# Last 256 tokens of the closing FFN as rows, and a reordered first layer, in a two-layer streaming encoder step

## The chip, the cores and the metric

The kernel runs on one core of one Trainium2 chip. The metric is the device time of one execution in microseconds (us); the time before is the median of 3 runs, 1388.47 us (1387.64 to 1388.97). The profile shows one execution, of 1387.13 us, whose span from the first to the last instruction is 1385.4 us.

The core's engines have queues of their own and wait for each other by semaphores: PE (matrix products; its weight loads are shown as PEld), DVE (vector), ACT (scalar and table functions), POOL, and SP, which here only issues DMAs. Each works its instructions off in the order in which the program wrote them.

## What is computed

576 tokens of 1024 features (64 of a running stream, then 512 of a new one) go through two layers. Layer 0 is a mixer of two head groups, mLSTM and retention, behind one input projection; layer 1 is a latent attention. Each is followed by a SwiGLU FFN, and after every sub-layer stands a norm of the residual. Cut to what matters here:

```
def layer(x):
    x = layer_norm(ALPHA * x + mixer(x), g_mix, b_mix)
    return layer_norm(ALPHA * x + swiglu(x), g_ffn, b_ffn)

def mixer_ab(x):                      # layer 0
    mq, mk, mv, mo, mif, rq, rk, rv, rg = split(x @ w_in)
    h = mlstm(mq, mk, mv, gates(mif))     # per chunk of tokens, state carried on
    o = retention(rope(rq), rope(rk), rv) # the same
    return concat(head_norm(h) * sigmoid(mo), head_norm(o) * silu(rg)) @ w_out

def swiglu(x):
    g, u = split(x @ w_gu)
    return (silu(g) * u) @ w_down
```

All is float32. The norm subtracts the mean over the 1024 features, divides by the root of the variance, and applies gain and bias.

## The kernel before

**Products.** A product is split into three: with each operand as a high and a low part in the rounded 32-bit type, it is high x high, low x high and high x low. So each weight and each activation exists twice (`Xh`, `Xl` for the input of a stage, `H` with its high and low halves for the input of a down or output projection). ACT writes the high part by a cast (L364), DVE the low part by a subtraction (L362).

**Weights.** The class `Plan` lays all weight pieces one after the other into blocks of 128 x 1024 (512 KB). SP brings a block into one of three raw buffers (`dma_w`, L342; a fourth is there for the FFN's own blocks); a block is called in as soon as a raw buffer's old contents have been split. Half a block (512 columns) is a *fill*: it is split into a ring *slot* when its order comes. That order is made by `prefetch(i, lead)`: whenever the program is about to use fill i, it first writes the splits of the fills up to i + lead, as far as their blocks are called in and a slot is free. Some fills have a slot of their own (`pins`). Since each engine works in program order, a split that is ordered early also stands early in the queues of ACT and DVE, ahead of what is written later.

**Order of the work.** It is written out by the program itself: main units of products follow each other, and between them `tick()` lets background tasks (norms, recurrences) emit their next step when a modelled PE clock has reached their due time (`LAG`).

**Token halves and tiles.** Feature-major products (`fm`) hold 320 or 256 tokens as columns (`HN`): weights stand, activations stream, and the output has features as partitions. Token-major products (`tm`) take a tile of 128 tokens (64 for the first) as the standing operand and stream 512 weight columns. Results come into PSUM banks: 3 for main products (`mm`), 4 for side work (`x`), 1 more (`o`).

**The first layer up to the mLSTM.** `setup` orders x of the first 320 tokens into `Z` and the first weight blocks: tiles 0 and 1 of x singly, then pairs. `layer0` splits x (L600, L601) and runs tiles 1 and 2 of the projection rq,rk as x arrives. x of the other 256 tokens is ordered at k = 3 and 4, after the constants (L752 to L754: rope, identity, mask, and the gate weights). At k = 7 that second half is split, ahead of the evacuations with rope of tiles 1 and 2 (`ev_qk`, L697 to L704). Then come gate products of the first half, tile 0 and tile 3 of rq,rk, gate products of the second half, tile 4, and the token-major projections rv and mv. `gates` (L829 to L911) works out the mLSTM's stabilisers in steps, with transposes on PE in between, and ends with four small products that spread the decays. `retention` works tile by tile in three steps: scores times a decay mask (`s1`, L928), output and state update, then the norm over each head (`s2`, L950 to L970), and transposes of the result (`s3`). `s1` uses the one `o` bank and an `mm` bank. The feature-major projections from `mk` on begin when the last `s3` has been written. All ten slots of `L0_SLOTS` are shared by the projections' fills, and rq,rk's eight are held until its last tile.

**The end.** The closing FFN works its inner dimension in three parts (8, 7 and 7 tiles of 128); the last part's down projection runs as eight feature units per half (`down_units`), of 7 x 3 products each, five units of the first half ahead of the second's first (`chain`). Each unit's bank is added to `Z` (L1187). The norm works on features as partitions: an early mean estimate by a product with ones (`ln_c`), sums and squares per unit (L1209 to L1233), then statistics by products, a root by seven small DVE steps (L539 to L543), a diagonal matrix to spread it (L1261), and per feature tile a subtraction, a scaling and a bias (L1265, L1279, L1298, L1321). The tail of the second half shares this among DVE, ACT and POOL, and stores (L1283).

Of the kernel before, what the change touches and what calls it, by code (L numbers as in the profile page):

```python
# [42 lines left out]
FILL = 512  # L43
SKEW = 5
# [4 lines left out]
L0_SLOTS = (0, 1, 2, 3, 4, 5, 6, 7, 14, 15)  # L49
# [63 lines left out]
def weight_pieces():  # L113
# [58 lines left out]
class Plan:  # L172
# [4 lines left out]
    def __init__(self):  # L177
        self.blocks, self.fills, self.where, self.quads, self.quad_blocks = [], [], {}, {}, set()
        used, at, left = BLK, FILL, 0
        for p in weight_pieces():  # L180
# [23 lines left out]
            self.where[p[0]] = (len(self.fills) - 1, at, w)  # L204
            used += w
# [12 lines left out]
class Kern:  # L218
    def __init__(self, ctx, tc, t):
# [18 lines left out]
        self.done, self.late_lo = set(), None  # L238
        for li in range(2):
# [86 lines left out]
    def slot(self, s):  # L326
        b = self.buffer(s)
# [97 lines left out]
    def prefetch(self, i, lead, qlead=QLEAD):  # L425
        last = len(self.plan.fills) - 1
        self.load()
        while True:
# [3 lines left out]
            if j > min(i + (lead if j > last or len(self.plan.fills[j]) == 3 else qlead), last):  # L432
                return
# [120 lines left out]
    def setup(self):  # L554
# [42 lines left out]
    def split_x(self, half, ks):  # L597
        for k in ks:
            a, b = hcols(half, k)
            self.nc.scalar.copy(self.Xh[:, a:b], self.Z[:, a:b])  # L600
            self.nc.vector.tensor_tensor(self.Xl[:, a:b], self.Z[:, a:b], self.Xh[:, a:b].bitcast(F32), ALU.subtract)  # L601
# [20 lines left out]
    def layer0(self):  # L622
# [41 lines left out]
        def tm_units(name, evac, tiles=range(NT)):  # L664
# [72 lines left out]
        banks = [None, self.bank(), self.bank()]  # L737
        for k in range(KT):
# [16 lines left out]
            if k in (3, 4):  # L755
                j = k - 3
                nc.sync.dma_start(half_view(Z, 1, 4 * j, 4 * j + 4), half_dram(t["x"], 1, 4 * j, 4 * j + 4))
# [5 lines left out]
        tm_units("rqrk", ev_qk, (0,))  # L763
        tm_units("rqrk", ev_qk, (3,))
# [3 lines left out]
        tm_units("rqrk", ev_qk, (4,))  # L768
        tm_units("rv", ev_rv)
# [9 lines left out]
        tm_units("mv", ev_mv)  # L779
# [1484 lines left out]
```

## Time and profile before

| | |
|---|---|
| median of 3 runs | 1388.47 us (1387.64 to 1388.97) |
| profiled execution | 1387.13 us |
| its span | 1385.4 us |
| busy: PE, DVE, ACT, POOL | 97%, 71%, 44%, 11% of the span |
| PE waits for DVE T L1226 (late in the span) | 3.8 us in two waits |
| PE waits for ACT Z L1318 (norms between stages) | 3.6 us in two waits |
| DMA | 112.91 MB, mean 81 GB/s |

A row of the timeline gives the start in us, the duration, engine, line of the kernel, operation, the output and inputs by their names in the program, their shape, and how many instructions of one kind follow each other; in brackets stands the idle time of the engine before them and what ended it. A row of the waits gives who waited for whom, us in total, how often, and the longest. A row of the windows gives a stretch, its length, then busy time and instructions of PE, PEld, DVE, ACT and POOL, the clock that PE was granted, and share and rate of DMA. A row of the DMA table gives the count, the size, and the median us from issue to landing. The ends of matmuls are modelled.

### The profile page before, as it was taken

The numbers are of one execution on the slowest core, as the hardware profiler recorded it, in microseconds if no ns is written. First come the engines' busy times: TensorE is split into PE (matmuls) and PEld (weight loads), VectorE is DVE, ScalarE is ACT, GpSimd is POOL, SyncE is SP. The second block draws the span as 40 slices with busy tenths as digits, with TensorE's granted clock in tenths as the row PEclk, the third lists the DMA queues.
The fourth block names the chain that finished last, engine by engine and source line by source line (L and its number), as shares of the span: only waits on it lengthen the run. The fifth ranks groups of instructions, "written<-read, shape, count | busy, mean of one in ns | idle before, by whom it ended". The sixth has DMA issues, their size and how long they took to land.

```text
span 1385.4 us, 24616 instructions
## 1 busy us (share of the span) xinstructions
PE 1348.3 (97%) x9759; PEld 1302.8 (94%) x9759; DVE 978.6 (71%) x2277; ACT 612.1 (44%) x1295; POOL 154.8 (11%) x182
## 2 busy tenths in 40 slices
PE   8999999999999999999999999999999999999995
PEld 6778999999999999999988899999999999999995
DVE  6666777678873685588898666667787358647877
ACT  4422333445551453255355466644555135425533
POOL 1100001115000000000021533311310000000000
PEclk9999999999999999999999999999999999999997
DMA  6111122511232123222322011130313312222221
GB/s 219 61 62 60 53 65 64 191 60 62 91 107 78 62 99 113 78 92 91 123 85 60 31 31 32 31 107 31 92 62 115 100 62 92 92 92 77 94 75 69
DMA packets 38235, 112.91 MB, mean 81 GB/s; under 512 B 5025, under 2 KB 12513, under 8 KB 38121
## 3 DMA queue, kind: packets, MB, share of 16 engines
q1 hardware_dynamic: 38120, 111.35, 24.4%
q8 instruction: 76, 1.25, 0.4%
q14 instruction: 39, 0.31, 0.1%
HBM read 107.45 MB, written 3.89 MB: 80 GB/s over the span
## 4 chain that ended last, share of the span: by engine, by line
PE 81%; DVE 12%; ACT 3%; DMA 2%; issue 2%; POOL 0%; SPq 0%; POOLq 0%; ACTq 0%; DVEq 0%
PE mm L465 42%; PE x L465 36%; DVE r L362 2%; PE x L533 2%; DVE Z L1279 1%; DMA raw<-in_w 1%; DVE Z L1265 1%; PE o L465 1%; ACT r L364 1%; ACT Xh L1311 1%; ACT Z L1318 0%; DMA Z<-in_x 0%; DVE small L543 0%; DVE small L542 0%; DVE small L541 0%
## 5 line engine op out<-in xcount | busy, mean ns | idle before, releaser
L465 PE MATMUL mm<-H,r 128*128 128x320 f32 (+2 forms) x2832 | 386.5, 296 | 0.0
L465 PEld LDWEIGHTS mm<-H,r 128*128 128x128 f32 x2832 | 377.2, 188 | 0.5 <-issue 0.2
L465 PE MATMUL x<-Xh,r 128*128 128x288 f32 x1216 | 244.7, 295 | 0.0
L465 PE MATMUL mm<-Xh,r 128*128 128x288 f32 (+2 forms) x1152 | 230.3, 298 | 6.0 <-DVE Z L1185 2.9
L364 ACT CAST r<-raw 128x512 fp32r<-128x512 f32 (+2 forms) x292 | 178.6, 648 | 104.9 <-PE mm L465 75.9
L362 DVE TENSOR_TENSOR r<-raw,r 128x512 fp32r<-128x512 f32 (+2 forms) x276 | 194.4, 734 | 37.7 <-ACT r L364 37.5
L465 PE MATMUL x<-r,r 128*128 128x288 f32 (+2 forms) x1534 | 211.7, 293 | 0.2 <-DVE r L1055 0.2
L465 PEld LDWEIGHTS x<-r,r 128*128 128x128 f32 x1534 | 205.9, 188 | 0.7 <-DVE r L1055 0.5
L465 PEld LDWEIGHTS x<-Xh,r 128*128 128x128 f32 x1216 | 194.5, 188 | 0.5
L465 PEld LDWEIGHTS mm<-Xh,r 128*128 128x128 f32 x1152 | 184.5, 190 | 7.2 <-ACT Z L1318 3.8
L465 PE MATMUL x<-Xl,r 128*128 128x288 f32 x608 | 179.2, 295 | 0.0
L465 PE MATMUL mm<-Xl,r 128*128 128x288 f32 (+2 forms) x576 | 167.5, 299 | 0.0
L364 ACT CAST r<-T 128x512 fp32r<-128x512 f32 (+1 forms) x114 | 87.1, 764 | 127.8 <-DVE T L397 109.1
L465 PEld LDWEIGHTS x<-Xl,r 128*128 128x128 f32 x608 | 114.0, 188 | 0.0
L362 DVE TENSOR_TENSOR r<-T,r 128x512 fp32r<-128x512 f32 (+1 forms) x114 | 96.3, 866 | 19.0 <-ACT r L364 19.0
L465 PEld LDWEIGHTS mm<-Xl,r 128*128 128x128 f32 x576 | 107.8, 190 | 0.1
L465 PE MATMUL mm<-r,Xh 128*128 128x512 f32 (+1 forms) x320 | 97.1, 385 | 4.4 <-DVE r L699 1.8
L1319 POOL TENSOR_TENSOR Xl<-Z,Xh 128x288 fp32r<-128x288 f32 (+2 forms) x36 | 30.9, 861 | 466.9 <-ACT Z L1318 466.4
L465 PEld LDWEIGHTS mm<-r,Xh 128*128 128x128 f32 x320 | 57.6, 188 | 17.3 <-issue 2.2
L1223 ACT ACTIVATE T<-Z 128x288 f32<-128x288 f32 (+2 forms) x56 | 24.9, 445 | 91.5 <-DVE Z L1185 47.1
L465 PE MATMUL mm<-r,Xl 128*128 128x512 f32 (+1 forms) x160 | 60.5, 378 | 0.0
L1580 DVE TENSOR_TENSOR T<-T,x 128x288 f32<-128x288 f32 x38 | 17.3, 454 | 58.7 <-PE x L465 58.7
(316 smaller groups left out, 1723.3 us busy)
## 6 DMA issues: line engine op xcount, KB each, us to landing
raw<-in_w SPq DMA_DIRECT2D x169, 512.0 KB, 3.5
r<-in_w SPq DMA_DIRECT2D x20, 512.0 KB, 3.5
Z<-in_x SPq DMA_DIRECT2D x1, 1280.0 KB
o_y<-Z SPq DMA_DIRECT2D x2, 640.0 KB, 3.3
Z<-in_x SPq DMA_DIRECT2D x2, 512.0 KB, 6.2
Z<-in_x SPq DMA_DIRECT2D x1, 1024.0 KB, 8.8
o_y<-Z SPq DMA_DIRECT2D x4, 256.0 KB, 2.1
Z<-in_x SPq DMA_DIRECT2D x3, 320.0 KB, 4.7
```

What stands on the lines that cost most here:

```text
L362: self.lo_engine.tensor_tensor(t[:, 1], src, t[:, 0].bitcast(F32), ALU.subtract)
L364: self.nc.scalar.copy(t[:, 0], src)
L465: self.nc.tensor.matmul(out, lhsT, rhs, start=start, stop=stop, skip_group_check=more)
L533: self.nc.tensor.transpose(out, in_, self.ident[0:n, 0:n])
L1223: nc.scalar.activation(q, z, AF.Square)
L1265: V.tensor_tensor(z, z, xd[:, 0:n], ALU.subtract)
L1279: V.scalar_tensor_tensor(z, z, gain(m), R[:, 0:n], ALU.mult, ALU.mult)
L1311: A.activation(self.Xh[:, a:b], z, AF.Identity, bias=bias(m))
L1319: G.tensor_tensor(self.Xl[:, a:b], z, self.Xh[:, a:b].bitcast(F32), ALU.subtract)
L1580: V.tensor_tensor(s[:, 0:n], s[:, 0:n], ps, ALU.add)
```

## The change

Eight things are changed.

1. The last down projection's second half (256 tokens) is computed by rows. Its weights are laid out as 14 pieces of 512 columns (`dt`), which the first half's feature units read in parts of 128. All eight units of the first half run first. Then two tiles of 128 tokens follow, each in two groups of 512 features: four plain float32 products with the identity put the residual from `Z` into the bank, and 21 products add to it. The norm of the row tile is taken straight from the banks: statistics by BN_STATS, mean subtracted on ACT, scaling and bias by DVE (the first tile's bias by POOL). Gain and bias come by a DMA that repeats 8 KB on all partitions (1 MB). The output has an array of its own.
2. In this stage the fills are ordered eight ahead (`FILLS_T`).
3. x of the first half comes in single tiles up to tile 3, and the second weight block in two parts; x of the second half is ordered at k = 1, ahead of the constants, into a free tile.
4. Tiles 1 and 2 of rq,rk are evacuated before the second half of x is split.
5. The fills of rq,rk and mv get eight slots in `H`; a cap (`self.cap`) spreads how far ahead fills are ordered: rv's during rq,rk, mv's during rv, mk's during mv.
6. The gates' decay products come 4.5 later on the modelled clock.
7. In the retention the scores of tile i + 2 come between output and norm of tile i, and the second tile's scores use an `x` bank instead of `o`.
8. `mk` begins when the last `s2` has been written, not the last `s3`.

```diff
+FILLS_T = 8
-L0_SLOTS = (0, 1, 2, 3, 4, 5, 6, 7, 14, 15)
+L0_SLOTS = (6, 7, 14, 15, 0, 1, 2, 3, 4, 5)
...
+            if (li, f1) == (1, FT):
+
+                for g in range(2):
+                    for k in range(f0, f1):
+                        out.append(((("dt", g), k), "w_down", li, k * 128, [(512 * g, 512)]))
+                continue
...
+        for k in range(KT):
+            for nm in ("rqrk", "mv"):
+                self.pins[self.where[(nm, k)][0]] = (len(RING) + k,)
...
+        if s >= len(RING):
+            o = 2 * FILL * (s - len(RING))
+            return self.H[:, o:o + 2 * FILL].rearrange("p (e c) -> p e c", e=2)
...
-            if j > min(i + (lead if j > last or len(self.plan.fills[j]) == 3 else qlead), last):
+            if j > min(i + (lead if j > last or len(self.plan.fills[j]) == 3 else qlead), last, max(i, self.cap)):
...
-            for k in (2 * j, 2 * j + 1) if j == 0 else (2 * j,):
-                e = k + 1 if j == 0 else k + 2
+            for k in (2 * j, 2 * j + 1) if j < 2 else (2 * j,):
+                e = k + 1 if j < 2 else k + 2
                 nc.sync.dma_start(half_view(self.Z, 0, k, e), half_dram(t["x"], 0, k, e))
                 if j < RAW and k % 2 == 0:
-                    self.dma_w(j, 2 if j == 0 else 1)
+                    self.dma_w(j, 2 if j < 2 else 1)
...
+                    self.cap = self.where[(name, KT - 1)][0] + ahead * (1 if len(tiles) == 1 else i + 1)
...
         for k in range(KT):
-            self.lead = 1 - k % 2 if k < KT - 1 else LEAD
+            self.lead = 1 - k % 2
             self.split_x(0, [k])
             if k == KT - 1:
                 self.split_wg()
-                self.split_x(1, range(KT))
...
-                if k == KT - 1:
-                    ev_qk(i, banks[i])
-            if k == 3:
+            if k == 1:
+                for j in range(2):
+                    nc.sync.dma_start(x1[:, 4 * j:4 * j + 4, :], half_dram(t["x"], 1, 4 * j, 4 * j + 4))
                 for name in ("rope", "ident", "mask", "cst"):
...
+        for i in (1, 2):
+            ev_qk(i, banks[i])
+            self.split_x(1, range(4 * i - 4, 4 * i), x1)
...
         gate_mm(0)
-        tm_units("rqrk", ev_qk, (0,))
-        tm_units("rqrk", ev_qk, (3,))
+        self.lead = 2 * KT
+        tm_units("rqrk", ev_qk, (0,), 2)
+        tm_units("rqrk", ev_qk, (3,), 5)
         gate_mm(1)
...
-        tm_units("rqrk", ev_qk, (4,))
-        tm_units("rv", ev_rv)
+        tm_units("rqrk", ev_qk, (4,), 8)
+        tm_units("rv", ev_rv, ahead=2)
...
-        tm_units("mv", ev_mv)
+        tm_units("mv", ev_mv, ahead=2)
+        self.cap, self.lead = len(self.plan.fills), LEAD
...
-                self.wait(lambda: self.ret_at["s3"] == NT)
+                self.wait(lambda: self.ret_at["s2"] == NT)
...
+        yield 4.5
+        x3 = self.xbank()
+        for h in range(4):
+            self.mm(x3[:, h * 8:h * 8 + 5], self.sel[:, h * 128:(h + 1) * 128], dec, True, True)
...
-            for o, bank in enumerate((self.obank(), self.bank())):
+            for o, bank in enumerate((self.xbank() if i == 1 else self.obank(), self.bank())):
...
-            s2(i)
+            O = s2(i)
+            if i + 2 < NT:
+                s1(i + 2)
+            s2b(i, O)
...
-        self.chain(down_units(p, f0, f1), ahead)
+        if not last:
+            self.chain(down_units(p, f0, f1), ahead)
+            return
+
+        gb, rows = (self.st(x, [128, KT * NTOK]) for x in ("Xh", "Xl"))
+        nc.sync.dma_start(gb[:, 0:2048], self.t["lnt"].to_broadcast([128, 2048]))
+        gb = gb[:, 0:2048].rearrange("p (e f) -> p e f", e=2)
+        self.rel, self.lead = False, FILLS_T
+        for _, d in down_units(p, f0, f1):
+            d(0)
+            self.tick()
+        for i in range(2):
...
+            banks = [self.bank(), self.obank() if i else self.bank()]
+            for g, ps in enumerate(banks):
+                for j in range(4):
+                    z = (4 * g + j) * NTOK + c
+                    self.mm(ps[:, 128 * j:128 * j + 128], Z[:, z:z + 128], self.ident, j == 0, False, more=True)
+                for k in range(f0, f1):
+                    wh, wl = self.wget((("dt", g), k))
+                    o = (k - f0) * NTOK + c
+                    xh, xl = H[:, o:o + 128], H[:, LO + o:LO + o + 128]
+                    self.mm(ps, xh, wh, False, False, more=True)
+                    self.mm(ps, xh, wl, False, False, more=True)
+                    self.mm(ps, xl, wh, False, k == f1 - 1, more=True)
+                    if k % 2:
+                        self.tick()
+                V.bn_stats(bs[:, g, :], ps)
+            V.bn_aggr(mv, bs)
+            V.tensor_scalar(nm, mv[:, 0:1], -1.0, None, ALU.mult)
+            y = [rows[:, (2 * i + g) * 512:(2 * i + g + 1) * 512] for g in range(2)]
+            for g, ps in enumerate(banks):
+                A.activation(y[g], ps, AF.Identity, bias=nm)
+            V.tensor_scalar(ve, mv[:, 1:2], LN_EPS, None, ALU.add)
+            self.rsqrt(rs, ve, None, tt)
+            for g in range(2):
+                V.scalar_tensor_tensor(y[g], y[g], rs, gb[:, 0, 512 * g:512 * g + 512], ALU.mult, ALU.mult)
+                (V if i else G).tensor_tensor(y[g], y[g], gb[:, 1, 512 * g:512 * g + 512], ALU.add)
+                nc.sync.dma_start(self.t["o_yt"][i, :, 512 * g:512 * g + 512], y[g])
```

More of the change, by code (lines that the diff above doesn't have):

```diff
@@ L204, in __init__ @@
             self.where[p[0]] = (len(self.fills) - 1, at, w)
+            if p[0][0][0] == "dt":
+                for j in range(4):
+                    self.where[(("d", 1, 4 * p[0][0][1] + j), p[0][1])] = (len(self.fills) - 1, at + 128 * j, 128)
             used += w
@@ L238, in __init__ @@
         self.done, self.late_lo = set(), None
+        self.cap = len(self.plan.fills)
+        for k in range(KT):
+            for nm in ("rqrk", "mv"):
+                self.pins[self.where[(nm, k)][0]] = (len(RING) + k,)
         for li in range(2):
@@ L595, in split_wg, with split_x @@
         self.nc.vector.tensor_tensor(self.wgp[:, :, 8:16], wg, hi.bitcast(F32), ALU.subtract)
-    def split_x(self, half, ks):
+    def split_x(self, half, ks, src=None):
         for k in ks:
             a, b = hcols(half, k)
-            self.nc.scalar.copy(self.Xh[:, a:b], self.Z[:, a:b])
-            self.nc.vector.tensor_tensor(self.Xl[:, a:b], self.Z[:, a:b], self.Xh[:, a:b].bitcast(F32), ALU.subtract)
+            x = self.Z[:, a:b] if src is None else src[:, k, :]
+            self.nc.scalar.copy(self.Xh[:, a:b], x)
+            self.nc.vector.tensor_tensor(self.Xl[:, a:b], x, self.Xh[:, a:b].bitcast(F32), ALU.subtract)
     def xs(self, half, cut=HN[0]):
@@ L662, in layer0, with tm_units @@
         half_sum = Z[0:64, 3972:4484]
-        def tm_units(name, evac, tiles=range(NT)):
+        def tm_units(name, evac, tiles=range(NT), ahead=LEAD):
             for i in tiles:
@@ L737, in layer0 @@
         banks = [None, self.bank(), self.bank()]
+        x1 = T1[:, 0:KT * HN[1]].rearrange("p (k t) -> p k t", k=KT)
         for k in range(KT):
-            self.lead = 1 - k % 2 if k < KT - 1 else LEAD
+            self.lead = 1 - k % 2
             self.split_x(0, [k])
@@ L901, in gates @@
         V.tensor_copy(dec[:, 1:5], stk[32:36, 191::128])
-        x1, x2, x3 = self.xbank(), self.xbank(), self.xbank()
+        x1, x2 = self.xbank(), self.xbank()
         for i in range(1, NT):
@@ L905, in gates @@
         self.transpose(x2[0:64, 0:128], stk[:, 0:64])
-        for h in range(4):
-            self.mm(x3[:, h * 8:h * 8 + 5], self.sel[:, h * 128:(h + 1) * 128], dec, True, True)
         nc.gpsimd.memset(self.tc_[:, 0], 0.0)
@@ L959, in s2, with s2b @@
                         V.scalar_tensor_tensor(to, up, dec, to, ALU.mult, ALU.add)
+            return O
+        def s2b(i, O):
+            L = TLEN[i]
             bs = self.smalls(24).rearrange("p (h c) -> p h c", h=4)
@@ L987, in task @@
         def task(i):
-            while at["s1"] < i or at["s2"] < i - 1 or self.qk_done < NT:
-                yield
-            s1(i)
-            at["s1"] += 1
-            yield LAG["r1"]
+            if i < 2:
+                while at["s1"] < i or self.qk_done < NT:
+                    yield
+                s1(i)
+                at["s1"] += 1
+                yield LAG["r1"]
             while at["s2"] < i or at["s3"] < i - 1:
@@ L1668, in ffn @@
         self.use_slots(RING)
-        self.chain(down_units(p, f0, f1), ahead)
+        if not last:
[9 more added lines that the diff above has]
+        for i in range(2):
+            c = HN[0] + 128 * i
+            bs = self.smalls(12).rearrange("p (g c) -> p g c", g=2)
+            mv = self.smalls(2)
+            nm, ve, tt, rs = (self.smalls(1) for _ in range(4))
+            banks = [self.bank(), self.obank() if i else self.bank()]
+            for g, ps in enumerate(banks):
+                for j in range(4):
+                    z = (4 * g + j) * NTOK + c
[21 more added lines that the diff above has]
+                nc.sync.dma_start(self.t["o_yt"][i, :, 512 * g:512 * g + 512], y[g])
     def layer1(self):
@@ L2225, in host_inputs @@
     d["lnv"] = ln.transpose(3, 0, 1, 2)
+    d["lnt"] = np.concatenate([a["ln_ffn_g"][1], a["ln_ffn_b"][1]])[None, :]
     d["gq"] = np.concatenate([a["g_q"][0], a["g_kv"][0]])[None, :]
@@ L2234, in host_outputs @@
     import numpy as np
-    y = np.concatenate([r["o_y"][:, :8 * 320].reshape(128, 8, 320), r["o_y"][:, 8 * 320:].reshape(128, 8, 256)], 2)
-    y = y.transpose(2, 1, 0).reshape(NTOK, D_MODEL)
+    y = np.concatenate([r["o_y"].reshape(128, 8, 320).transpose(2, 1, 0).reshape(320, D_MODEL),
+                        r["o_yt"].reshape(256, D_MODEL)], 0)
     out = [y[64:], y[:64]]
```

5 lines of the change are left out of this document (1 added, 4 removed).

## The prediction

> **What bounds the kernel now.** I read the page first, then the waits of PE, then the timeline of PE at both ends of the program, since the change touches only the first 125 us and the last 65.
>
> ```profile
> span 1385.4 us, 24616 instructions
> PE 1348.3 (97%) x9759; PEld 1302.8 (94%) x9759; DVE 978.6 (71%) x2277; ACT 612.1 (44%) x1295; POOL 154.8 (11%) x182
> ```
>
> PE carries a record for 97% of the span, so there are only two ways to gain: less matmul work, or fewer of the 37 us in which PE has nothing. The waits of PE say where those are (us in total, times, longest):
>
> ```profile
> PE o L465 <- DVE r L928: 2.7, 2, 1.4
> PE mm L465 <- DVE r L699: 1.8, 1, 1.8
> PE mm L465 <- DVE r L362: 1.4, 2, 1.2
> PE mm L465 <- ACT r L364: 1.2, 1, 1.2
> PE x L533 <- DVE r L702: 0.4, 1, 0.4
> PE mm L533 <- DVE r L970: 0.3, 1, 0.3
> ```
>
> All six lie in the first layer. The rest is the tail, where the timeline of PE and of ACT (start, duration) shows:
>
> ```profile
> 1320.14 9.40 PE L465 MATMUL mm<-H,r 128*128 128x320 f32 x63
> 1329.38 0.32 PE L465 MATMUL x<-Z,ones 128*128 128x320 bf16 x1
> 1354.30 5.21 PE L465 MATMUL mm<-H,r 128*128 128x256 f32 x42
> 1359.35 0.78 PE L465 MATMUL x<-T,ones 128*128 128x128 f32 x6
> 1359.93 7.70 PE L465 MATMUL mm<-H,r 128*128 128x256 f32 x63
> 1379.99 1.80 ACT L1298 ACTIVATE Z<-Z,lnv 128x256 f32<-128x256 f32 x4 [0.88 <-POOL Z L1291]
> ```
>
> The last product ends at 1359.93+7.70 = 1367.6. The span ends at 1385.4, so 17.8 us follow in which the last half is normed on DVE, POOL and ACT and stored; of these 1385.4-1381.8 = 3.6 us come after the last ACT operation (the store).
>
> **The end: rows instead of columns.** The half of 256 tokens keeps its multiply work but turns it: 8 units x 21 products of 256 columns become 2 tiles x 2 groups x 21 products of 512. The 42 products from 1354.30 to 1359.35 take 0.120 us each, so 168 cost 20.2 us. A 512-wide product is seen in the first layer, and so are the plain f32 products that bring the residual into the bank by the identity (two records each):
>
> ```profile
> 67.46 0.63 PE L465 MATMUL mm<-r,Xh 128*128 128x512 f32 x2
> 67.93 0.39 PE L465 MATMUL mm<-r,Xl 128*128 128x512 f32 x1
> 68.16 0.63 PE L465 MATMUL mm<-r,Xh 128*128 128x512 f32 x2
> 84.83 1.05 PE L465 MATMUL x<-T,r 128*128 128x128 f32 x8
> 85.81 0.71 PE L465 MATMUL x<-T,Z 64*128 64x128 f32 x8
> ```
>
> Between 67.46 and 68.16 lie three products: 0.233 each, so 84 cost 19.6 us. Four plain products of 128 columns take 85.81-84.83 = 0.98, so 16 cost 3.9 us. (The six records at 1359.35, three products in 0.58, give 0.19 each and 3.1 us: the low bound.) PE's last product therefore moves by 19.6+3.9-20.2 = +3.3, to 1370.9. The statistics products of the other half's norm stay as they are.
>
> What follows the last product becomes short: one BN_STATS over 512, an aggregate, a negated mean, eps and the seven steps of the root, then four 512-wide operations and the store. ACT's two mean subtractions run beside the root.
>
> ```profile
> 88.49 0.88 DVE L964 BATCH_NORM_STATS2 small<-x 64x6 f32<-64x128 f32 x4
> 89.40 0.38 DVE L966 BATCH_NORM_AGGREGATE small<-small 64x2 f32<-64x6 f32 x4
> 90.01 0.16 DVE L539 TENSOR_SCALAR small<-small 64x4 int32<-64x4 int32 x1
> 91.16 0.16 DVE L543 SCALAR_TENSOR_TENSOR small<-small 64x4 f32<-64x4 f32 x1
> 25.25 0.69 DVE L697 TENSOR_TENSOR r<-mm,rope 128x512 f32<-128x512 f32 x1
> ```
>
> BN_STATS over 512 isn't in the trace: no less than one of 128 (0.22), no more than four (0.88); I take 0.65, near the 0.69 of the 512-wide row. Aggregate 0.1, negation 0.2, root and eps 0.2+(91.32-90.01) = 1.5, four operations at 0.69 less overlap 2.7, hand-over from PE 0.1 (an estimate): 5.3. With the store's 3.6 the tail is 8.9 instead of 17.8. Net: 8.9-3.3 = 5.6 us gained, 5.4 to 6.8 by these bounds. The other half's norm now hides under the row tiles, which last 19.6+3.9 = 23.5 us; the first row tile's norm and POOL's two bias adds hide under the second.
>
> Against it stands the order of the 14 splits. The lead of 8 puts all of them on ACT and DVE before the first product of the stage, so ahead of the first evacuation, and the 1 MB broadcast of gain and bias is put on the SP queue ahead of the last weight block.
>
> ```profile
> L342 SPq DMA_DIRECT2D raw<-in_w x1: 328/328/328, 1324.6 to 1324.6; - x1
> 1325.04 2.42 ACT L364 CAST r<-raw 128x512 fp32r<-128x512 f32 x4 [1.47 <-DMA raw<-in_w]
> 1326.31 0.88 DVE L1187 TENSOR_TENSOR Z<-Z,mm 128x320 f32<-128x320 f32 x2
> 1336.63 1.29 DVE L362 TENSOR_TENSOR r<-raw,r 128x512 fp32r<-128x512 f32 x2 [0.25 <-ACT r L364]
> 1294.00:1296.00 2.00, 2.00 (x17) 2.00 (x16) 2.00 (x4) 0.00 (x0) 0.00 (x0) 1.00 0.95 387
> raw<-in_w SPq DMA_DIRECT2D x169, 512.0 KB, 3.5
> ```
>
> Today the last block is issued at 1324.6 (it waits until splits 6 and 7 have read their buffer), its two splits run at 1336.6, and the first two evacuations go ahead of them at 1326.3. Afterwards they go behind. The block lands at 1324.6+3.5 = 1328.1 without the broadcast; blocks 4 and 5 land about 1325 to 1326 by the ACT row, the broadcast takes 1.05 MB at 387 GB/s = 2.7, the block 1.4 more: about 1330.2 with it. Two splits (0.6 of ACT until DVE can follow, a quarter of 2.42, then 1.3) and one evacuation (0.5) end at 1330.5 or 1332.6. PE wants that evacuation at 1329.38 (the mean product of the norm). It waits 1.1 to 3.2 us; I take 2.8, since the broadcast is issued first. [...] The end gives 5.6-2.8 = 2.8.
>
> **The first layer.** x by single tiles: today the third tile's products wait 1.2 for its weights. Smaller pieces bring tiles 2 and 3 earlier, but the gate products follow directly behind tile 7, and their weights now land later.
>
> ```profile
> 16.80 0.25 ACT L594 CAST wgp<-T 128x64 fp32r<-128x64 f32 x1 [2.02 <-DMA T<-in_wg]
> 17.08 0.23 DVE L595 TENSOR_TENSOR wgp<-T,wgp 128x64 fp32r<-128x64 f32 x1 [1.11 <-ACT wgp L594]
> 18.66 0.31 PE L465 MATMUL x<-Xh,wgp 128*16 128x320 f32 x1
> 15.00:20.00 5.00, 5.00 (x27) 3.72 (x26) 1.46 (x4) 0.95 (x4) 1.03 (x2) 1.00 0.88 265
> ```
>
> On the queue 1 MB of x (second half) now precedes the gate weights where a 0.5 MB block did: 0.52 MB at 387 to 265 GB/s is 1.4 to 2.0 us, so the gate weights are ready at 18.7 to 19.3 instead of 17.3. The gain at the start is swallowed: -0.1 (bounds -0.6 to 0).
>
> What goes: the two evacuations with rope no longer stand behind the split of the late second half of x (L699 1.8, L702 0.4). rqrk's weights get slots in H, so rv's eight splits are done before rv starts (the 1.2 of L362; its other 0.2 stays). The scores of tile i+2 precede the norm of tile i on DVE, so their bank is emptied before the norm, and the second tile gets its own bank (L928 2.7). mk starts without the last norm (L970 0.3). Sum 6.4. A wait counts from the modelled end of the last record. Two 512-wide records take 0.63 and the second starts 0.233 after the first, so one is 0.40 long, and the next could have started 0.16 before its end: 0.16 more for each of six, together 7.4.
>
> What comes: eight splits and the second half of x now stand in DVE's queue ahead of the gates' first stage, whose result ten transposes wait for.
>
> ```profile
> 19.73 1.43 DVE L601 TENSOR_TENSOR Xl<-Z,Xh 128x256 fp32r<-128x256 f32 x4 [2.43 <-ACT Xh L600]
> 37.48 0.42 DVE L704 TENSOR_TENSOR Z<-r,cst 128x256 f32<-128x256 f32 x1
> 39.85 0.16 DVE L829 TENSOR_TENSOR small<-x,bif 64x8 f32<-64x8 f32 x1 [1.96 <-issue]
> 42.96 0.18 DVE L849 TENSOR_TENSOR small<-small 128x20 f32<-128x20 f32 x1
> 45.27 1.24 PE L533 MATMUL x<-ident,small 64*4 64x64 f32 x10
> 85.00:120.00 35.00, 33.73 (x207) 27.86 (x207) 28.85 (x125) 4.72 (x9) 0.35 (x2) 1.00 0.00 1
> ```
>
> The four evacuations (first row at 25.25, above) take 25.25 to 37.90 = 12.65 without a gap. After the change DVE starts them at 18.7, and 2.9 of x and 8x0.65 = 5.2 of splits come between: 39.4, and with the gates' 3.3 (39.85 to 43.14) 42.7. PE arrives at the transposes at 45.27 less the waits gone by then (1.8+0.4 and 0.3 of uncounted) = 42.3 to 42.8 with the 0.1 above: a wait of 0.4 (0 to 2). The decay products, 4.5 later, are needed only by the mLSTM: nothing. First layer: 7.4-0.4-0.1 = 6.9.
>
> **Sum.** 6.9+2.8 = 9.7. The profiled execution took 1387.13 (span 1385.4 and 1.7 around it), so 1377.4; the median of the runs lies 1.34 above it: 1388.47-9.7 = **1378.8**.
>
> **The rivals.** *DVE becomes the bound of the first layer.* From 85 to 120 it is busy 28.85 of 35. The change takes one wait on L928 (1.4) out of that stretch and puts six to eight early splits (3.9 to 5.2) in: 32.8 to 34.0 in 33.6. Then the state update of the fourth tile comes too late for the fifth, and about 3 of the 7.4 come back as waits: 1381.8. For it speaks the fullness of DVE, against it that PE has a whole tile of mv (24x0.233 = 5.6) between two retention steps to run ahead.
>
> *The rows give nothing.* The wait for the last block is 5.6 rather than 2.8, if the broadcast runs at half the rate of weights: 1388.47-6.9 = 1381.6. No wide broadcast of this size is in the trace.
>
> *The early order doesn't happen.* A fill is skipped when its block has not been called in or its slot is held; then rv still waits 1.4 with its uncounted part: 1380.1. For it: there are still three raw buffers for blocks; against it, eight slots more.
>
> *Slower: the splits dam up the vector queue.* A split ordered ahead of its block's landing stops DVE, and the evacuation behind it. In the first layer 13 tiles order splits at their start, with three raw buffers. If each stop lasts d, 13d less the 6.1 of free DVE time above must exceed 9.7+2.8 before the kernel is slower by 0.2%: from d = 1.4 on. A landing takes 3.5. With d = 2, 26-6.1-9.7 = +10.2: 1398.7. Against it: mostly two splits, one block's worth, are ordered per tile, and the two other buffers can fill meanwhile.
>
> **How the numbers follow.** My forecast 0.50, DVE bound 0.23, rows give nothing 0.12, no early order 0.07, slower 0.06; 0.02 remains for better than forecast. The range reaches down to all waits gone and the upper bound of the end with no stop (1388.47-7.4-6.8 = 1374.3) and up to both middle rivals together, 1388.47-3.9 = 1384.6: 1374.5 to 1385.0. About 0.2% (2.8 us) is what a measurement tells from no change. Faster by more 0.87, within 0.07 (rivals adding up), slower 0.06.
>
> **What would show it.** Right: the waits on L699, L928 and L970 are gone, and the one on L362 is at most 0.2; the gate products start at 18.6 to 19.3; PE's last product ends about 1366.8 (1370.9+2.8-6.9) and 8.9 us follow it; one wait of 1 to 3 us on DVE Z early in the last stage. Wrong: a longer tail than 11 us, plain products dearer than 0.25, waits of the retention products on DVE updates, a wait over 4 on the last blocks, or PE idle at the row tiles.

## The result and the profile after

The changed kernel takes 1378.85 us (median of 4 runs, 1377.22 to 1379.03) against 1388.72 us (4 runs) for the kernel before on the same chip: ratio 0.9928, 95% interval 0.9916 to 0.9940, about 9.9 us less. The forecast was 1378.8. The sum came out; its two large terms did not.

First the page of the changed kernel, then its waits of PE (us in total, times, longest). Line numbers are now those of the changed kernel.

```profile
span 1377.0 us, 24436 instructions
PE 1348.6 (98%) x9692; PEld 1302.6 (95%) x9692; DVE 971.5 (71%) x2251; ACT 606.2 (44%) x1283; POOL 154.7 (11%) x180
```

```profile
PE x L482 <- DVE Z L1219: 3.7, 1, 3.7
...
PE x L550 <- DVE small L871: 0.5, 1, 0.5
PE x L482 <- DVE wgp L612: 0.3, 1, 0.3
```

All six waits that the prediction listed are gone from the first layer, but for twice 0.2 on splits of weights (L379, L381), of the kind that was expected to stay. Two small ones are new there (the gate transposes, the gate weights), and one large one in the last stage. The windows from the first product of the input projection to the first product of mk show the first layer, before and then after (start and end, length, then busy time of PE, PEld, DVE, ACT, POOL):

```profile
4.87:122.34 117.47, 109.64 (x568) 85.10 (x569) 83.56 (x254) 40.59 (x80) 9.39 (x24) 1.00 0.29 94
```

```profile
4.93:112.39 107.46, 106.31 (x564) 84.95 (x565) 84.42 (x244) 41.67 (x84) 9.19 (x24) 1.00 0.36 119
```

PE without a record fell from 117.47-109.64 = 7.8 to 1.15 us, and PE's recorded time by 3.3 more. Of the 10.0 some 0.5 is only moved (the last transposes of the retention now lie behind mk's start). The last stage begins at 1311.25 instead of 1320.14, so 8.9 us earlier. But from there to the end of the span it takes 1377.0-1311.25 = 65.75, where it took 65.26. **The rows gave nothing; the first layer gave all of it.** The timeline of PE in the last stage of the changed kernel shows where the rows' gain went:

```profile
1311.25 9.40 PE L482 MATMUL mm<-H,r 128*128 128x320 f32 x63
1324.31 0.42 PE L482 MATMUL x<-Z,ones 128*128 128x320 bf16 x1 [3.67 <-DVE Z L1219]
1324.34 18.26 PE L482 MATMUL mm<-H,r 128*128 128x320 f32 x105
1342.43 1.05 PE L482 MATMUL mm<-ident,Z 128*128 128x128 f32 x8
1343.24 2.34 PE L482 MATMUL mm<-r,H 128*128 128x512 f32 x9
...
1363.12 5.15 PE L482 MATMUL o<-r,H 128*128 128x512 f32 x21
```

PE stands for 3.67 us (3.84 with the uncounted part) at the first evacuation. The 63 products ahead of it start 0.147 apart; at that rate the 105 behind it would take 15.6, but they take 18.26. The four plain products take 1343.24-1342.43 = 0.81, and behind the last product (1363.12+5.15 = 1368.27) follow 8.7 us.

The queues of SP, ACT and DVE show what PE stands for:

```profile
1312.72 0.41 SPq L1706 DMA_DIRECT2D Xh<-in_lnt  x1
1315.66 0.33 SPq L359 DMA_DIRECT2D raw<-in_w  x1
```

```profile
1321.92 1.14 ACT L381 CAST r<-raw 128x512 fp32r<-128x512 f32 x2 [2.60 <-DMA raw<-in_w]
```

```profile
1322.57 1.29 DVE L379 TENSOR_TENSOR r<-raw,r 128x512 fp32r<-128x512 f32 x2 [2.45 <-ACT r L381]
1323.78 1.27 DVE L1219 TENSOR_TENSOR Z<-Z,mm 128x320 f32<-128x320 f32 x3
```

The broadcast of gain and bias is issued 2.9 ahead of the last weight block; the block lands 6.3 after its issue, where a block takes 3.5 (median of all); its two splits go first on DVE, and only then the evacuation that PE wants.

The windows of the same stretch show the other half (the figure 1.00 or 0.50 is PE's granted clock):

```profile
1319.83:1323.24 3.41, 0.81 (x6) 0.65 (x5) 0.96 (x3) 1.14 (x2) 0.00 (x0) 1.00 0.18 72
1323.24:1326.66 3.42, 2.35 (x9) 2.35 (x9) 3.38 (x9) 0.87 (x2) 0.00 (x0) 0.50 0.00 0
1326.66:1330.07 3.41, 3.41 (x14) 3.41 (x14) 2.91 (x8) 0.47 (x1) 0.00 (x0) 0.50 0.00 0
1330.07:1333.48 3.41, 3.41 (x24) 3.41 (x24) 1.38 (x4) 0.47 (x1) 0.00 (x0) 1.00 0.00 0
```

During the stop PE's clock is halved, for twice 3.41 us, and the first 21 products behind the stop take 0.267 each instead of 0.147: 2.5 us that the prediction didn't know of. The stop cost 6.3 in all, more than the 5.6 that the rows were to bring.

### The profile page after: what moved, and what is told of

Same layout as the page of the kernel before. It is cut to its first block, busy times and chain, and to the rows that moved or that the text cites. A ratio compares the mean times of both kernels' runs of the same rounds, so it can differ in the third digit from the quotient of the medians.

```text
span 1377.0 us, 24436 instructions
## 1 busy us (share of the span) xinstructions
PE 1348.6 (98%) x9692; PEld 1302.6 (95%) x9692; DVE 971.5 (71%) x2251; ACT 606.2 (44%) x1283; POOL 154.7 (11%) x180
## 4 chain that ended last, share of the span: by engine, by line
PE 84%; DVE 9%; DMA 3%; ACT 3%; issue 1%; POOL 0%; SPq 0%; ACTq 0%; DVEq 0%; POOLq 0%
PE mm L482 44%; PE x L482 36%; DMA raw<-in_w 2%; DVE r L379 2%; PE x L550 2%; PE o L482 1%; DVE Z L1311 1%; DVE Z L1297 1%; ACT r L381 1%; ACT Xh L1343 1%; DMA Z<-in_x 0%; ACT Z L1350 0%; DMA T<-in_wg 0%; DVE Xl L619 0%; DVE small L559 0%
## 5 line engine op out<-in xcount | busy, mean ns | idle before, releaser
L482 PE MATMUL mm<-H,r 128*128 128x256 f32 (+2 forms) x2664 | 368.8, 298 | 0.0
L482 PEld LDWEIGHTS mm<-H,r 128*128 128x128 f32 x2664 | 359.7, 189 | 4.2 <-issue 3.9
L381 ACT CAST r<-raw 128x512 fp32r<-128x512 f32 (+2 forms) x276 | 168.8, 648 | 98.6 <-PE mm L482 73.3
L379 DVE TENSOR_TENSOR r<-raw,r 128x512 fp32r<-128x512 f32 (+2 forms) x260 | 183.5, 734 | 25.7 <-ACT r L381 25.3
L381 ACT CAST r<-T 128x512 fp32r<-128x512 f32 (+1 forms) x114 | 86.9, 762 | 127.0 <-DVE T L414 114.7
L379 DVE TENSOR_TENSOR r<-T,r 128x512 fp32r<-128x512 f32 (+1 forms) x114 | 96.3, 865 | 18.4 <-ACT r L381 18.4
L482 PE MATMUL mm<-r,H 128*128 128x512 f32 (+3 forms) x323 | 60.3, 339 | 0.1
L1255 ACT ACTIVATE T<-Z 128x288 f32<-128x288 f32 (+2 forms) x49 | 21.9, 447 | 83.5 <-DVE Z L1217 47.6
L482 PE MATMUL mm<-r,Xh 128*128 128x512 f32 (+1 forms) x192 | 55.2, 371 | 0.9 <-ACT Z L1350 0.9
L1641 DVE SCALAR_TENSOR_TENSOR Z<-Z,mm 128x320 f32<-128x320 f32 (+1 forms) x32 | 14.3, 453 | 59.3 <-PE mm L482 59.3
## 6 DMA issues: line engine op xcount, KB each, us to landing
Z<-in_x SPq DMA_DIRECT2D x1, 1024.0 KB, 8.7
Xh<-in_lnt SPq DMA_DIRECT2D x1, 1024.0 KB
```

The lines of the kernel that those rows point to most:

```text
L379: self.lo_engine.tensor_tensor(t[:, 1], src, t[:, 0].bitcast(F32), ALU.subtract)
L381: self.nc.scalar.copy(t[:, 0], src)
L482: self.nc.tensor.matmul(out, lhsT, rhs, start=start, stop=stop, skip_group_check=more)
L1255: nc.scalar.activation(q, z, AF.Square)
L1641: V.scalar_tensor_tensor(z, z, ALPHA, ps[:, 0:HN[half]], ALU.mult, ALU.add)
```

## The experiments

Theory: the end's gain went into the stop, which two edits make together (the broadcast ahead of the last block, and that block's splits ahead of the evacuations), and into the slow clock behind it; the first layer's gain is that of its removed waits. Each group ran with the kernel before on its own chip (medians 1387.3 to 1389.0), so ratios compare best; "last stage" is from its first product to the end of the profiled span.

| kernel | us | ratio to before, 95% | last stage |
|---|---|---|---|
| before | 1388.72 | | 65.26 |
| changed | 1378.85 | 0.9928 (0.9916 to 0.9940) | 65.75 |
| broadcast late | 1375.62 | 0.9902 (0.9887 to 0.9916) | 60.68 |
| broadcast late, five ahead | 1375.84 | 0.9905 (0.9890 to 0.9920) | 61.48 |
| five ahead | 1374.46 | 0.9896 (0.9881 to 0.9910) | 61.43 |
| half the broadcast late | 1376.62 | 0.9911 (0.9894 to 0.9928) | 63.44 |
| first layer alone | 1379.36 | 0.9937 (0.9922 to 0.9952) | 65.56 |
| old retention | 1380.75 | 0.9946 (0.9932 to 0.9961) | 64.46 |
| no slots in H | 1380.65 | 0.9950 (0.9934 to 0.9966) | 63.99 |
| old input | 1381.61 | 0.9951 (0.9934 to 0.9967) | 65.67 |
| end alone | 1386.06 | 0.9994 (0.9980 to 1.0008) | 64.24 |
| both repairs | 1373.15 | 0.9897 (0.9884 to 0.9911) | 59.35 |
| old mk and decay products | 1388.11 | 1.0003 (0.9994 to 1.0013) | 64.55 |
| both repairs, pool adds | 1373.97 | 0.9906 (0.9893 to 0.9920) | 59.68 |

### What makes the stop

**Broadcast late.**

```diff
-        nc.sync.dma_start(gb[:, 0:2048], self.t["lnt"].to_broadcast([128, 2048]))
...
         for _, d in down_units(p, f0, f1):
             d(0)
             self.tick()
+        nc.sync.dma_start(gb[:, 0:2048], self.t["lnt"].to_broadcast([128, 2048]))
```

> Only the broadcast of gain and bias moves, behind the first half's units. Theory (the stop of the last stage ate the gain of the rows, half of it made by the broadcast ahead of the last weight block, and the long stop brought a stretch of 0.50 clock with it): the last block, issued 4.4 after the stage's start, lands 3.5 later and not 6.3; from landing to PE's restart it was 2.4; so PE stops about 1.1 instead of 3.84, the clock stays near 1, and the 21 products behind the stop take 0.147 and not 0.267 each (2.5). Sum -5.3: about 1373.6 us. Rival 1 (the splits ahead of the evacuations alone make the stop): the stop stays above 3 and the time within 1 us of 1378.9. Rival 2 (the slow products have nothing to do with the length of the stop): the stop goes, the slow stretch stays, 1376.1.

PE in the last stage:

```profile
1322.29 0.30 PE L482 MATMUL x<-Z,ones 128*128 128x320 bf16 x1 [1.16 <-DVE Z L1219]
1322.32 15.67 PE L482 MATMUL mm<-H,r 128*128 128x320 f32 x105
```

The stop is 1.16, the 105 products take 15.67, the stage is 5.07 shorter than in the changed kernel. Both rivals fall by the trace: the stop is not above 3, and no slow stretch stands behind it. The time alone would not tell: it fell by 3.2 by the medians and 3.6 by the ratios, not by 5.3, and 1375.62 lies nearer to the 1376.1 of rival 2 than to 1373.6. (The profiled execution, 1374.20, is the fastest of the four.)

**Five ahead** (the broadcast stays early) and **broadcast late, five ahead**.

```diff
-FILLS_T = 8
+FILLS_T = 5
```

> Only the order of the splits: five ahead, the broadcast still ahead of the last block. Theory (the stop needs both the late block and its splits ahead of the evacuations; either one undone removes most of it): the block is needed only from the fifth unit on, 12 us after the stage's start, and lands after 10.6; no stop, no slow stretch, about 1372.6 us. Rival 1 (the broadcast alone is what stops PE, by the DMA queue or by its writes): the stop stays above 3, about 1378.9.

> The broadcast late and the fills ordered five ahead instead of eight, so that the last block's two splits stand behind the first four evacuations. Theory: no stop over 0.5 in the last stage, no slow stretch: 3.84 + 2.5 = 6.3 less, about 1372.6 us. Rival 1 (the splits ahead of the evacuations alone make the stop): the same time as with five ahead and the broadcast early. Rival 2 (slow stretch independent of the stop): 1375.1.

The stop at the first evacuation is gone in both, so the order of the splits alone suffices as well. With five ahead the place of the broadcast makes no difference (61.48 and 61.43, as rival 1 of the second had it); with eight ahead it is worth 2.5 us of stop. But neither reached 1372.6: both stages are some 2 us longer than the changed kernel's less 6.3, and by the same rows (PE, five ahead, broadcast early):

```profile
1320.26 5.55 PE L482 MATMUL mm<-H,r 128*128 128x320 f32 x36
1326.88 0.41 PE L482 MATMUL mm<-H,r 128*128 128x320 f32 x1 [1.07 <-ACT r L381]
1327.61 2.63 PE L482 MATMUL mm<-H,r 128*128 128x320 f32 x15 [0.31 <-DVE r L379]
```

Five ahead orders the last block's splits only when the fifth unit begins, behind the norm's steps for the fourth on ACT and DVE: 1.07 and 0.31 are waited there. Too late is the same fault as too early, with another sign.

**Half the broadcast late.**

```diff
-        nc.sync.dma_start(gb[:, 0:2048], self.t["lnt"].to_broadcast([128, 2048]))
+        nc.sync.dma_start(gb[:, 0:1024], self.t["lnt"][:, 0:1024].to_broadcast([128, 1024]))
...
+        nc.sync.dma_start(gb[:, 1024:2048], self.t["lnt"][:, 1024:2048].to_broadcast([128, 1024]))
```

> Half of the broadcast (the gain) ahead of the last block, the other half late. Theory: half the bytes, so the block lands half of 2.8 earlier, and the stop is 3.84 - 1.4 = 2.4. If the slow stretch comes only behind a stop that is long enough, and 2.4 is short enough (no stop of 2.4 in the trace has one, the one of 3.84 has), the clock stays up and the gain is 1.4 + 2.5 = 3.9: about 1375.0 us. Rival 2 (the slow stretch does not depend on the length of the stop): 21 products at 0.267 remain, and the gain is 1.4: 1377.5.

The stop's size came as expected, 2.52. With 1.16 without a broadcast ahead and 3.67 with all of it, each of the two halves (0.52 MB) cost 1.2 to 1.4: the stop grew with the bytes issued ahead of the block. But the clock did not stay up, as I had expected from a stop of 2.5. (The changed kernel's own trace already held a wait of 2.6 with a slow window behind it, near 296 us; it is shown below.) The windows:

```profile
1319.95:1323.36 3.41, 0.89 (x8) 0.72 (x6) 1.82 (x4) 1.14 (x2) 0.00 (x0) 1.00 0.29 118
1323.36:1326.78 3.42, 3.42 (x14) 3.42 (x14) 3.39 (x9) 1.34 (x3) 0.00 (x0) 0.50 0.00 0
1326.78:1330.19 3.41, 3.41 (x25) 3.41 (x24) 2.97 (x8) 0.47 (x1) 0.00 (x0) 1.00 0.00 0
```

The slow stretch is there, but 3.41 long instead of 6.83, and costs 1.5 instead of 2.5. Nor does rival 2 hold, since its length changed. In both, the window of 3.41 us in which PE worked only 0.81 or 0.89 us stands just ahead of the slow one. Here PE restarted at 1323.29 and worked all of the next window (3.42), and the clock was 1.00 after it; in the changed kernel the next window held 1.07 more of the stop (2.35 worked), and a second slow one followed.

**Both repairs**: the broadcast late, and

```diff
-        for _, d in down_units(p, f0, f1):
+        for m, (_, d) in enumerate(down_units(p, f0, f1)):
+            self.lead = LEAD if m < 2 else FILLS_T
             d(0)
             self.tick()
```

> The changed kernel with the broadcast behind the first half's units and the fills five ahead for the first two units, then eight: the last block's splits stand behind two evacuations and are still early for the fifth unit. Theory: neither the stop at the first evacuation (3.84) nor the slow stretch (2.5) nor the wait of 1.1 and 0.7 that five ahead brought at the fifth unit: the last stage lasts 65.75 - 6.3 = 59.5 us, the kernel 1372.6. Rival (some stop has to remain, since the last block's weights cannot be had earlier): a last stage of 60.7 to 61.5 as with either repair alone, 1374 to 1375.

```profile
1320.89 0.32 PE L482 MATMUL x<-Z,ones 128*128 128x320 bf16 x1
1320.93 15.67 PE L482 MATMUL mm<-H,r 128*128 128x320 f32 x105
...
1357.13 5.15 PE L482 MATMUL o<-r,H 128*128 128x512 f32 x21
```

No stop is left, and the stage is 59.35, 5.9 shorter than before the change: what the rows are worth when nothing takes it back. At 1373.15 us it beats both kernels (against the changed one by medians 5.7, by ratios 0.0031 or 4.3; the clock had two slow windows ahead of the last stage in this profile and one in the changed kernel's). That it beats five ahead alone is shown by the last stage only (59.35 against 61.43); the ratios, 0.9897 and 0.9896, are the same.

**Both repairs, pool adds**: the last tile's first bias addition goes to POOL.

```diff
-                (V if i else G).tensor_tensor(y[g], y[g], gb[:, 1, 512 * g:512 * g + 512], ALU.add)
+                (V if i and g else G).tensor_tensor(y[g], y[g], gb[:, 1, 512 * g:512 * g + 512], ALU.add)
```

> As the kernel with both repairs, and the bias of the last tile's first 512 features is added by the pool engine instead of the vector engine. Theory: the four steps behind the root (0.75, 0.69, 0.74, 0.69 in a row) become three, and the pool engine's 1.47 (half of 2.93 for two) runs beside the other two: 0.6 less, last stage 58.9, 1372.0 us. Rival (pool and vector engine slow each other, or the pool engine's add ends last): no gain, 1372.6 or more.

```profile
1365.35 1.42 DVE L1741 SCALAR_TENSOR_TENSOR Xl<-Xl,small,Xh 128x512 f32<-128x512 f32 x2
1366.18 1.70 POOL L1742 TENSOR_TENSOR Xl<-Xl,Xh 128x512 f32<-128x512 f32 x1 [8.61 <-DVE Xl L1741]
1366.80 1.63 DVE L1742 TENSOR_TENSOR Xl<-Xl,Xh 128x512 f32<-128x512 f32 x1
```

The rival: DVE's addition took 1.63 beside POOL's, where it took 0.69 with both repairs, and the stage came out no shorter (59.68).

### The two halves of the change by themselves

**First layer alone**: without `FILLS_T`, the `dt` pieces and the rows. **End alone**: only these.

> The first layer's changes alone, with the last down projection in columns as before. Theory (the whole gain is made in the first layer, the end gives nothing): the same time as the changed kernel, 1388.7 - 9.5 = 1379.2 us; the first layer's lead over the kernel before stays at 9.5 near 250 us. Rival, the prediction's own terms (first layer 6.9, end 2.8): 1381.8.

> The end's changes alone (rows for the last 256 tokens, eight ahead, the broadcast early), on the first layer as it was. Theory (the stop of 3.8 and the slow stretch behind it eat what the rows bring): the last stage lasts 65 to 66 us as in the changed kernel, and the time is that of the kernel before within 1 us, 1388.5. Rival, the prediction's own terms (5.6 less a stop of 2.8): 2.8 less, 1385.8.

The first layer alone gives 0.9937 (8.7 us), within the noise as much as the whole change. The rival's 6.9 us would be 0.9950, which lies just inside the interval, so the times alone do not exclude it; the trace does, with 9.5 us less in the first layer (next section). The end alone gives 0.9994, with no change inside its interval and the prediction's 2.8 (0.9980) at its edge. In its profile the stop is 3.34 and one slow window follows, not two, hence 64.24 and not 65 to 66: 1.0 less than before the change, about the 5.9 of the rows less 3.5 for the stop and some 1.5 for the window (as with half the broadcast late). So the theory's cause is seen in the trace, and its sizes were a little too large.

### The parts of the first layer

Each part is undone in the changed kernel. The start varies between executions of the same code (gate products at 18.20 to 18.89), so I measure from the first gate product to the first product of mk. Before the change mk starts at

```profile
122.34 0.54 PE L465 MATMUL mm<-Xh,r 128*128 128x320 f32 x2
```

and 122.34-18.66 = 103.68. PE of the changed kernel:

```profile
18.20 0.32 PE L482 MATMUL x<-Xh,wgp 128*16 128x320 f32 x1 [0.28 <-DVE wgp L612]
...
112.39 0.54 PE L482 MATMUL mm<-Xh,r 128*128 128x320 f32 x2
```

94.19, so 9.5 less; with the first layer alone it is 94.17.

**Old retention.**

```diff
-            for o, bank in enumerate((self.xbank() if i == 1 else self.obank(), self.bank())):
+            for o, bank in enumerate((self.obank(), self.bank())):
...
-            O = s2(i)
-            if i + 2 < NT:
-                s1(i + 2)
-            s2b(i, O)
+            s2(i)
...
```

> The changed kernel with the old retention: the scores of tile i + 2 again behind the norm of tile i, the second tile again in the o bank. Theory (each removed wait is a gain of its own size): the two waits on the scores' decay products come back, 2.7 + 2 x 0.16 = 3.0, all between 70 and 125 us: 1381.9 us. Rival (the parts hide each other: with H slots and early splits the vector engine gets to the scores in time by itself): under 1, 1379.5.

```profile
17.94 0.32 PE L482 MATMUL x<-Xh,wgp 128*16 128x320 f32 x1 [0.16 <-DVE wgp L612]
...
114.07 0.54 PE L482 MATMUL mm<-Xh,r 128*128 128x320 f32 x2
```

96.13: 1.9 more, not 3.0. The wait came back with 1.7 in total (it was 2.7): so the truth lies between theory and rival: the other parts had already removed some of it (which of them was not tried).

**No slots in H.**

```diff
-        for k in range(KT):
-            for nm in ("rqrk", "mv"):
-                self.pins[self.where[(nm, k)][0]] = (len(RING) + k,)
...
-L0_SLOTS = (6, 7, 14, 15, 0, 1, 2, 3, 4, 5)
+L0_SLOTS = (0, 1, 2, 3, 4, 5, 6, 7, 14, 15)
...
```

The cap and the leads that go with it are undone as well.

> The changed kernel without slots in H, without the cap, with the old order of slots. Theory (removed wait, and faster products from H): the wait of 1.2 for the split of rv's weights comes back, with 0.16, and 224 products of 512 columns take 0.233 again instead of 0.228, 1.1: together 2.5, 1381.4 us; products of rq,rk at 0.233. Rival 1 (the prediction's terms: the wait alone): 1.4, 1380.3. Rival 2 (the early splits are what keeps vector work off the retention too): over 4, 1383, with waits that the kernel before did not have.

```profile
18.89 0.32 PE L475 MATMUL x<-Xh,wgp 128*16 128x320 f32 x1
...
115.56 0.54 PE L475 MATMUL mm<-Xh,r 128*128 128x320 f32 x2
```

96.67: 2.5 more, the theory's figure, against 1.4 for the wait alone. The other 1.1 fits the products' own rate, which is told below; the run undid the slots, the cap and the order together, so it does not separate them.

**Old input.**

```diff
-            for k in (2 * j, 2 * j + 1) if j < 2 else (2 * j,):
+            for k in (2 * j, 2 * j + 1) if j == 0 else (2 * j,):
...
-        for i in (1, 2):
-            ev_qk(i, banks[i])
-            self.split_x(1, range(4 * i - 4, 4 * i), x1)
+                self.split_x(1, range(KT))
...
```

> The changed kernel with the old input: x in pairs, its second half ordered at k = 3 and 4 and split ahead of the two evacuations with rope. Theory: the waits of 1.8 and 0.4 come back with 2 x 0.16, the gate products start 0.45 later, and the new wait of the gate transposes (0.5) goes: 1.8 + 0.4 + 0.3 + 0.45 - 0.5 = 2.5, 1381.4 us. Rival (the prediction's terms: the start gains nothing, the first x tiles cost nothing): 2.1, 1381.0; what tells them apart is the start of the gate products, 18.7 or 18.2.

```profile
20.84 0.31 PE L482 MATMUL x<-Xh,wgp 128*16 128x320 f32 x1
...
115.98 0.54 PE L482 MATMUL mm<-Xh,r 128*128 128x320 f32 x2
```

95.14, 1.0 more, and 2.6 later at the gate products. About 1.5 of the 2.6 is a slow window from 12.3 us on, behind a wait of 1.6 for the third tile's weights; the kernel before had that wait (1.2) without a slow window. Of the expected waits of 1.8 and 0.4 only one came back, with 0.8 (PE on DVE r L721). So this part is worth 1 to 3.6 (3.2 by the ratios), and neither figure is confirmed.

**Old mk and decay products.** These are the two parts that the prediction priced at 0.3 and at nothing.

```diff
-                self.wait(lambda: self.ret_at["s2"] == NT)
+                self.wait(lambda: self.ret_at["s3"] == NT)
...
+        for h in range(4):
+            self.mm(x3[:, h * 8:h * 8 + 5], self.sel[:, h * 128:(h + 1) * 128], dec, True, True)
         nc.gpsimd.memset(self.tc_[:, 0], 0.0)
...
-        yield 4.5
-        x3 = self.xbank()
-        for h in range(4):
-            self.mm(x3[:, h * 8:h * 8 + 5], self.sel[:, h * 128:(h + 1) * 128], dec, True, True)
```

> The changed kernel with the old start of mk (behind the last transposes of the retention) and the gates' decay products at their old place. The three larger parts undone one by one cost 1.9, 2.3 and 2.0 to 3.6 us by their traces, of 9.5. Theory (each part gives its own wait): the wait on the norm's last product comes back, 0.3 + 0.16, and nothing else: 1379.4 us. Rival (what the three parts leave of the 9.5 sits here): 1.5 to 2 more, 1380.6.

Both expectations are far off: 1388.11, ratio 1.0003. Without these two the whole change is worth nothing. From the first gate product to mk it is 123.24-18.65 = 104.59, 10.4 more than in the changed kernel. DVE and PE show why:

```profile
62.15 1.29 DVE L379 TENSOR_TENSOR H<-raw,H 128x512 fp32r<-128x512 f32 x2 [0.23 <-ACT H L381]
63.47 0.14 DVE L922 COPY small<-T 4x1 f32<-4x1 f32 x1
63.54 0.15 DVE L923 COPY small<-T 4x4 f32<-4x4 f32 x1
```

```profile
59.74 0.71 PE L550 MATMUL x<-ident,T 128*128 128x128 f32 x5
...
63.75 1.87 PE L482 MATMUL x<-small,T 4*128 4x5 f32 x8 [3.30 <-DVE small L923]
...
122.16 1.43 PE L550 MATMUL mm<-ident,r 128*128 128x128 f32 x4 [2.74 <-DVE r L996]
```

The decay products need two tiny copies, and these stand on DVE behind six of the splits that the change orders early. PE stops for 3.30 and then runs at half clock for 6.8 us (its 512-wide products start 0.43 apart from 66.56 to 69.12, and 0.23 again from 70.36 on). In the changed kernel the same copies run at 63.03 and the products at 65.53, with projection products in between. The old start of mk makes a second stop of 2.74 (PE on DVE L996, the last norm of the retention) with a second slow stretch of 6.8 (mk's first products start 0.267 apart). DVE is busy for 20.51 of the 22 us from 100 to 122 there (18.17 in the kernel before), with three pairs of early splits among the retention's steps, where the kernel before has none. That these splits make the second stop is read from the queue; the two parts were not undone singly.

## Why the prediction was right or wrong

**The total** was right by luck, because two errors met: the first layer gave 9.5 rather than 6.9, the end -0.5 rather than 2.8. These make 9.0, where the medians differ by 9.9 and the two profiled executions by 8.3; the clock's slow windows between the two ends fall differently from execution to execution (in these two there is one each, at 978.40 before and at 299.24 after).

**Rows and tail: right.** Without the stop PE's last product ends (1357.13+5.15-1311.65) = 50.6 after the stage's start instead of 47.5: +3.1 (predicted 3.3; a plain product takes 0.20, not 0.245). 8.7 follow it (8.9). The 5.6 of the end was 5.9. One reading was too wide, without harm to the sum: beside the six waits and the tail, some 14 of the 37 idle us lie between the stages (3.6 on ACT Z L1318 among them), and of the 3.8 on DVE T L1226 only one wait of 2.1 is in the tail. The change touches none of these.

**The stop: the failed step.** The prediction had the mechanism and its place, and 2.8 us with an upper bound of 3.2. It measured 3.8, outside the 1 to 3 that was to be the sign of being right. The path from landing to PE was 2.4 as worked out; the block landed 0.6 later than the worst case. And a whole term was missing: the wait was priced by its length alone, but at half clock the products behind it cost 2.5 more. The kernel before had a long stretch at 0.50 in its tail, 14.4 us from 1370.93 on, where only a few small products of the norm (1.73 us of PE work) were left to slow down.

**First layer: the waits right, two terms missing.** All listed waits went (but for the 0.2 above), the new one at the gate transposes was 0.5 (0.4), the gate products start as before within their spread. Missing were the faster products with weights in H (about 1.1 to 1.4) and some 1.5 in gaps below the waits' list, which no run separates. The prediction added the removed waits one by one. Undone one by one, retention and H slots cost 1.9 and 2.5, the input 1.0 or more, and the last two parts together 10.4: more than the whole 9.5, so the parts don't add up.

**"Decay products: nothing" and "mk 0.3": right as differences, wrong as prices.** They remove no wait of the kernel before; they keep the early splits from making two new ones of 3.30 and 2.74. "Needed only by the mLSTM" looked at who waits for the products, not at what the products wait for.

**The rivals.** The rows gave nothing, but by a shorter wait than that rival's 5.6 and a slow clock. DVE did not become the bound: no wait of the retention on it remains. But it came near: the last norm ends on DVE at 116.2, 3.8 after mk has started, and with the old start of mk PE waited 2.74 for it. The slower case (splits damming DVE's queue) came true at two places: 3.67 at the last block, where DVE stood for the landing, and, where the cover was taken away, 3.30 at the decay products, where the splits stood for ACT's casts.

## What to carry to other kernels

Price a new wait on PE of the sizes seen here (2.5 to 3.8 us) at its length plus up to 2.5 for the slow products behind it, and look whether the next work is dense products. When splits or loads are ordered earlier, look for the small instructions that now stand behind them in the same queue (here 3.30 us of PE at the decay products), and move their users back by as much. Put a large transfer that is needed late behind the one that is needed next (here the stop fell from 3.67 to 1.16), and judge a part of a change by taking it away from the whole: a part that removes no wait can be what keeps the others' gain.

## What the hardware showed that was not expected

**The clock moves on a fixed grid.** All slow stretches inside the programs were 3.41 or 6.83 us. In the changed kernel they begin at 299.24 and 1323.24, and the one that lasts to the end at 1371.03: 1024.0 and 47.8 apart, which is 300 and 14 times 3.413. In the kernel before they begin at 978.40 and 1370.93, 392.5 or 115 times 3.413 apart. The grid's place differs between executions: a wait of 2.64 us between stages near 296 us was followed by a slow window in the changed kernel,

```profile
295.80:299.20 3.40, 0.98 (x7) 1.01 (x8) 3.33 (x8) 3.30 (x8) 2.56 (x4) 1.00 0.30 116
299.20:302.70 3.50, 3.50 (x17) 3.50 (x16) 3.47 (x8) 1.90 (x5) 0.90 (x1) 0.51 0.03 7
```

and by none with the broadcast late, where two windows shared it (2.00 of 3.40 busy from 294.0 on, 2.15 from 297.4 on). One such window at clock 0.50 costs up to 3.41 x 0.5 = 1.7 us (an estimate; with half the broadcast late it was 1.5). Seven profiles with the same code up to the last stage reach it between 1310.97 and 1312.72; less the start of their gate products, those with one slow window on the way take 1292.6 to 1293.1, those with two 1293.3 to 1294.2. Laid out on this grid, the fourteen profiles hold 5551 whole windows at full clock up to PE's last product. A slow one came after each of the 20 windows with less than 1.5 us of recorded PE work, after 10 of the 197 with 1.5 to 3.0, and after none of the others. Within the middle group recorded work alone does not decide: in the kernel before, 2.29 us (from 974.98 on) was followed by a slow window and 1.57 us (from 305.97 on) was not. What does decide there stays open.

**Weights in H stream faster.** Three products with weights in the ring take 53.70-53.00 = 0.70, three with weights in H 104.88-104.20 = 0.68 (changed kernel):

```profile
53.00 0.63 PE L482 MATMUL mm<-r,Xh 128*128 128x512 f32 x2
53.46 0.40 PE L482 MATMUL mm<-r,Xl 128*128 128x512 f32 x1
53.70 0.63 PE L482 MATMUL mm<-r,Xh 128*128 128x512 f32 x2
```

```profile
104.20 0.61 PE L482 MATMUL mm<-H,Xh 128*128 128x512 f32 x2
104.66 0.39 PE L482 MATMUL mm<-H,Xl 128*128 128x512 f32 x1
104.88 0.61 PE L482 MATMUL mm<-H,Xh 128*128 128x512 f32 x2
```

0.006 less for each of the some 240 products of rq,rk and mv is 1.4 at most. Why was not tried.

**POOL's and DVE's bias additions slowed each other** (both repairs, pool adds). DVE's takes 1.63 instead of 0.69; begun 0.62 behind POOL's, it ended 0.55 behind it. POOL's took 1.70, where two in a row take 2.93 in the changed kernel, so 1.47 each: 0.23 longer, although it began 0.59 before DVE's last scaling ended (1366.18 and 1365.35+1.42 = 1366.77). Why was not tried.
